# Two stacked products and a re-searched order in a one-core hybrid attention layer

## The chip, the cores and the metric

The kernel runs on one core of a Trainium2 chip. The metric is the time of one execution in microseconds (us), measured on the device; before the change the median of three runs is 308.2 us (308.15 to 308.23). Engines are named as the profile names them: PE is TensorE's matmul, PEld its loading of the stationary operand, DVE VectorE, ACT ScalarE, POOL GpSimd, SP SyncE, whose queue issues all the transfers here.

## The reference

One layer over x of 512 positions by 1024. After an RMS norm, one projection (1024 by 3420 columns) feeds two groups of eight heads of width 64, and one output projection and the residual end the layer. All in float32.

```
h = rms_norm(x, norm_gain);  proj = h @ w_in
# group A, two key groups g of four heads: three attentions share the queries
o_cmp = attend(qn, kc_cmp, vc_cmp)      # 31 compressed keys (blocks of 32, stride 16, through an MLP)
o_sel = attend(qn, ks_r, vs)            # blocks of 64 selected; 16 of 8 wanted, so all causal keys
o_win = attend(qn, kw_r, vw)            # window 512, so all causal keys
o_nsa = (g0*o_cmp + g1*o_sel + g2*o_win) * silu(z_n)
# group B: an indexer scores all keys, each query attends its best 128 causal keys
score = sum_h relu(qi_h . ki) * wi_h;   idx = top_k(score, 128)
o_dsa = attend(qd, kd[idx], vd[idx]) * silu(z_d)
out = x + concat(o_nsa, o_dsa) @ w_out
```

## The kernel before, in words

Every float32 operand of a matmul is split into two float32r parts, hi (the rounded value) and lo (what the rounding left), and a product is made as hi*hi + hi*lo + lo*hi, or with one exact side as two matmuls. The splitting of the weights is a cast on ACT and a subtraction on POOL (line L358); that of activations is a cast on ACT and a subtraction on DVE.

The projection is made in chunks of columns (C, B, Q1, Q2, D, Z0 to Z3; matmuls at L391 and L401), the output projection at L1268 (`out`). Attention goes by units: a unit is one kind (`n` group A, `d` group B), one block i of 128 query positions, one key group g, and for `n` one of three branches (0 compressed, 1 selected, 2 window). `n300` is kind n, i = 3, g = 0, branch 0. Inside a unit the queries stand as four row blocks b of 32 positions by four heads, 128 rows each. So row block b of query block i has 128 i + 32 b + 32 causal keys at most.

A unit runs so: scores `s_...` on PE (L1033), masked minimum on DVE (L1003), exponential on ACT (L1010), scaling on POOL (L1023) into `P_...`; then by tiles of 128 keys `transposed` turns P on PE into a bank `T_...` (L1054, four transposes of 128x128), casts it to `pth` on ACT (L1056) and subtracts it into `ptl` on DVE (L1057); `times_values` multiplies each of the two with the values on PE (L1068) into `on...` or `od...`. The values tile holds hi and lo side by side as 128 stationary columns, and `combine` adds the two halves.

Two tiles of this are the subject. First, the compressed branch: its P is 128 rows by 4 blocks by 32 keys. One transpose (L1045) makes a 128x128 bank whose rows are (block, key); DVE multiplies it with a block-diagonal mask `diag` into 128x512 (L1047), ACT casts (L1049), POOL subtracts (L1050), and two matmuls of 512 columns follow; the compressed values are held four times, once for every block. Second, the tile of 128 keys on the diagonal of a `d` unit, which is treated as every other tile, though blocks 0 and 1 have at most 64 keys in it.

The order on each engine is not that of the code: `set_order` takes the whole program, costs each instruction (`cost`), and lets list scheduling run forward and backward over it `ROUNDS` times; the order with the earliest planned end is fixed with dependencies. Buffers come from pools with tags: two tiles of one tag share memory, and the later waits for the last reader of the earlier. `arena` is one tile from which constants are carved; `cst` is the array of constants in DRAM. `tables` multiplies the rotary tables with a gain on POOL (L525, L526, tile `tab`); `rope` uses them; `nz` and `ny` are inverse norms made by a chain of small POOL operations (L417 to L424), and `dr_q` takes `nz` through DRAM to the layout of the softmax. `hid` is the hidden layer of the compression MLP, `kc_ps` its compressed keys on the way to `kn`, the stack of group A's keys.

Of the kernel before, what the change touches and what calls it, by code (L numbers as in the profile page):

```python
# [109 lines left out]
def set_order(tc):  # L110
# [66 lines left out]
    for k, i in enumerate(insts):  # L177
        acc = []
        for w, ap in aps(i):
            t = ap.bass_ap.tensor  # L180
# [4 lines left out]
            off += sum((n - 1) * st for st, n in dims[1:] if st < 0)
            acc.append((t.name, "PSUM" in str(getattr(t, "space", "")), w, p0, p0 + dims[0][1], off * size, end * size))
            if getattr(t, "tag", None):
                u = used.setdefault(t.name, [])
# [4 lines left out]
        for name, bank, w, p0, p1, a, b in acc:
            for j, w2, q0, q1, c, d in seen.get(name, ()):
                if (a <= d and c <= b) if bank else (w or w2) and a < d and c < b and p0 < q1 and q0 < p1:
                    (before if w or w2 or eng[j] != eng[k] else behind)[k].add(j)
# [113 lines left out]
def tile_hybrid_layer(ctx, tc, xT, x, ng, win, gains, peT, w1, b1, w2, wout, cst, out):  # L310
# [125 lines left out]

    tri = carve([S], BF16)
    nc.vector.memset(tri, 0.0)  # L440
# [71 lines left out]
    nc.gpsimd.tensor_copy(trib[:, 32:64], cs[:, C_TRIB:C_TRIB + 32])  # L512
    nc.gpsimd.tensor_copy(trib[:, S + 32:S + 64], cs[:, C_TRIB:C_TRIB + 32])
    nc.gpsimd.memset(trib[:, S + 64:S + 96], -NEG)
    ccos = cs[:64, C_CCOS:C_CCOS + HD]
# [4 lines left out]

    def tables(j, name):
        gn = gns[:, j, None, :]
        tab = work.tile([128, 2, NT, HD], F32, tag=f"tab{j}", name=f"tab{j}", bufs=1)
# [1 line left out]
        nc.gpsimd.tensor_tensor(c, cosd, gn[:, :, :HD].to_broadcast([128, NT, HD]), op=ALU.mult)  # L525
        nc.gpsimd.tensor_tensor(s, sind, gn[:, :, HD:].to_broadcast([128, NT, HD]), op=ALU.mult)  # L526
# [207 lines left out]
    diag = carve([4, 128], BF16)  # L734
    nc.gpsimd.memset(diag, 0.0)
    for h in range(4):
        nc.gpsimd.memset(diag[32 * h:32 * h + 32, h], 1.0)
# [60 lines left out]
    def hidden1(kv):  # L798
# [12 lines left out]
    def hidden2(kv):  # L811
        hid, uT = FSs[kv]
        if kv:
            for g in range(2):
                for half in range(2):
                    nc.tensor.matmul(hid[:, 384 + 64 * g:448 + 64 * g], uT[:, half, g].rearrange("p r c -> p (r c)"),
                                     w2t[:, kv, half], start=(half == 0), stop=(half == 1))
# [220 lines left out]
    def transposed(u, item, parts):  # L1038

        p = ps("T", "T_" + u.name)  # L1040
        ph = work.tile([128, 512], F32R, tag="pth", name="pth", bufs=TBUFS)
        pl = work.tile([128, 512], F32R, tag="ptl", name="ptl", bufs=TBUFS)
        if u.b == 0 and u.kind == "n":
# [3 lines left out]
            nc.vector.tensor_tensor(pd, p[:, None, :128].to_broadcast([128, 4, 128]), diag, op=ALU.mult)  # L1047
            pd = pd.rearrange("p h q -> p (h q)")
            nc.scalar.copy(ph, pd)  # L1049
            nc.gpsimd.tensor_tensor(pl, pd, ph.bitcast(F32), op=ALU.subtract)  # L1050
        else:
            blocks = item[0]
            for b, c in blocks:
                nc.tensor.transpose(p[:, b * 128:(b + 1) * 128], u.P[:, b, c:c + 128], ident)  # L1054
            cols = slice(128 * blocks[0][0], 512)
            nc.scalar.copy(ph[:, cols], p[:, cols])  # L1056
            nc.vector.tensor_tensor(pl[:, cols], p[:, cols], ph[:, cols].bitcast(F32), op=ALU.subtract)  # L1057
        parts.append((u, item, ph, pl))

    def times_values(u, item, *parts):  # L1060
# [5 lines left out]
        for cols, v in item[1]:  # L1066
            for x, pp in enumerate(parts):
                nc.tensor.matmul(o[:, cols], v, pp[:, cols], start=(first and x == 0), stop=(end and x == 1))  # L1068
# [261 lines left out]
    weave(att, "n002", [  # L1330
        queries("Q2", "q", 0, [1], "D", {0: hidden3(), 1: hidden1(1), 3: hidden2(1)},
                (e_first, lambda p, t: e_evac(p[:, 256:], t), lambda: norm_scale([ST["kd_raw"]], ST["ss_kd"]))),
        queries("D", "d", 3, [0, 1], "Z0"),
        kd_stack(),
    ], RA, X1, LEAD)
# [112 lines left out]
```

## Time and profile before

| what | before |
|---|---|
| median of three runs | 308.2 us |
| profiled execution, span from its first to its last instruction | 306.4 us |
| median less span | 1.8 us |
| PE busy | 301.3 us (98%), 1669 matmuls |
| PEld busy | 256.4 us (84%) |
| DVE / ACT / POOL busy | 261.0 (85%) / 240.7 (79%) / 235.4 us (77%) |
| chain that ended last, by engine | PE 86%, DVE 4%, ACT 4%, POOL 3%, DMA 2%, issue 1% |
| moved by DMA | 32.42 MB, mean 106 GB/s |
| TensorE clock granted | 0.999 of full |

The profile is of one execution, for which it gives the span alone; the 1.8 us to the median lie around the span. In rows of groups the columns are line, engine, operation, tiles (out<-in), shapes and count, then busy us and mean ns of one, then the engine's idle time just before and who ended it. Rows of a timeline give start us, us, engine, line. A matmul's duration holds its passage through the array, which overlaps with the next; what a matmul costs PE is the distance from its start to the next start.

### The profile page before, as it was taken

What the parts mean: (1) busy time and instruction counts of PE and PEld (TensorE: products, weight loads), DVE (VectorE), ACT (ScalarE), POOL (GpSimd) and SP (SyncE); (2) the same over time, 40 slices, a digit from 0 to 9 for tenths busy, and PEclk for the clock granted to TensorE, in tenths of its full rate; (3) what the DMA queues carried; (4) which work ended last, traced back from release to release, by engine and by line L of the source; (5) the groups of instructions that cost most, each with busy time, mean ns of one, the idle gap of its engine ahead of it and who ended that gap; (6) DMA issues with size and microseconds to landing.
All of it is one profiled execution on the core that took longest, in us unless ns stands there. A gap on an engine that the chain in (4) does not pass through costs nothing.

```text
span 306.4 us, 5994 instructions
## 1 busy us (share of the span) xinstructions
PE 301.3 (98%) x1669; PEld 256.4 (84%) x1669; DVE 261.0 (85%) x797; ACT 240.7 (79%) x802; POOL 235.4 (77%) x418
## 2 busy tenths in 40 slices
PE   8999999999999999999999999999999999999995
PEld 5997788899878878888888888888888888888885
DVE  4999699999979998998999999999769989986502
ACT  6965776798969999999989999774379998996400
POOL 3099899997996599987989879985667997686410
PEclk9999999999999999999999999999999999999999
DMA  7995345375410034310121023450443343003011
GB/s 282 415 356 181 96 147 163 92 187 158 114 28 0 0 79 125 106 57 3 38 68 39 3 72 106 136 165 0 141 125 120 106 141 103 4 14 122 20 50 68
DMA packets 21249, 32.42 MB, mean 106 GB/s; under 512 B 5664, under 2 KB 8480, under 8 KB 21216
## 3 DMA queue, kind: packets, MB, share of 16 engines
q1 hardware_dynamic: 21216, 32.05, 34.2%
q8 instruction: 13, 0.21, 0.3%
q14 instruction: 20, 0.16, 0.2%
HBM read 29.04 MB, written 2.47 MB: 103 GB/s over the span
## 4 chain that ended last, share of the span: by engine, by line
PE 86%; DVE 4%; ACT 4%; POOL 3%; DMA 2%; issue 1%; DVEq 0%; POOLq 0%
PE out L1268 15%; PE z L401 14%; PE Q L391 8%; PE D L391 7%; PE B L391 7%; PE on L1068 7%; PE s_n L1033 6%; PE T_n L1054 5%; PE od L1068 3%; PE T_d L1054 3%; PE s_d L1033 3%; PE C L401 2%; PE hid L787 2%; ACT hThi L467 2%; POOL wlo_Q L358 2%; PE idx L699 1%
## 5 line engine op out<-in xcount | busy, mean ns | idle before, releaser
L1010 ACT ACTIVATE P_n<-P_n,arena 128x416 f32<-128x416 f32 (+15 forms) x64 | 33.7, 528 | 4.7 <-DVE arena L1003 4.1
L1003 DVE CUSTOM_DVE_ANT_0 P_n<-s_n,arena 128x416 f32<-128x416 f32 (+15 forms) x64 | 31.0, 499 | 1.0 <-PE s_n L1033 0.4
L1023 POOL TENSOR_SCALAR P_n<-P_n,arena 128x416 f32<-128x416 f32 (+15 forms) x64 | 30.8, 501 | 1.2
L1057 DVE TENSOR_TENSOR ptl<-T_n,pth 128x512 fp32r<-128x512 f32 (+1 forms) x40 | 25.0, 627 | 3.6 <-ACT pth L1056 2.9
L1033 PE MATMUL s_n<-kn,arena_r 128*128 128x512 f32 (+11 forms) x104 | 27.1, 342 | 0.0
L710 DVE MAX8 m<-scores 128x8 f32<-128x512 f32 (+2 forms) x48 | 26.5, 552 | 0.6
L401 PE MATMUL z<-hThi,whi_Z 128*128 128x512 f32 x64 | 26.1, 408 | 0.0
L711 DVE MATCH_REPLACE8 scores<-m,scores 128x512 f32<-128x512 f32 (+2 forms) x48 | 26.0, 542 | 0.1
L401 PE MATMUL z<-hTlo,whi_Z 128*128 128x512 f32 x64 | 25.3, 396 | 0.0
L401 PE MATMUL z<-hThi,wlo_Z 128*128 128x512 f32 x64 | 25.2, 397 | 0.0
L1054 PE MATMUL T_n<-arena,P_n 128*128 128x128 f32 x144 | 24.1, 273 | 0.0
L1268 PE MATMUL out<-whi_wo,mx 128*128 128x512 f32 (+1 forms) x72 | 23.8, 374 | 0.0
L1268 PE MATMUL out<-wohi,mx 128*128 128x512 f32 (+1 forms) x72 | 23.7, 377 | 0.0
L1056 ACT CAST pth<-T_n 128x512 fp32r<-128x512 f32 (+1 forms) x40 | 21.5, 540 | 2.7 <-PE od L1068 1.6
L391 PE MATMUL Q<-whi_Q,hThi 128*128 128x256 f32 (+1 forms) x64 | 22.2, 347 | 0.6 <-DVE kn L587 0.6
L391 PE MATMUL Q<-wlo_Q,hThi 128*128 128x256 f32 (+1 forms) x64 | 21.9, 343 | 0.0
L391 PE MATMUL Q<-whi_Q,hTlo 128*128 128x256 f32 (+1 forms) x64 | 21.9, 344 | 0.0
L1054 PEld LDWEIGHTS T_n<-arena,P_n 128*128 128x128 f32 x144 | 18.1, 140 | 4.0
L1033 PEld LDWEIGHTS s_n<-kn,arena_r 128*128 128x128 f32 x104 | 18.1, 189 | 3.3 <-issue 0.2
L358 POOL TENSOR_TENSOR wlo_Z<-raw_Z,whi_Z 128x512 fp32r<-128x512 f32 x16 | 20.4, 1291 | 0.5 <-ACT whi_Z L357 0.5
L358 POOL TENSOR_TENSOR w1l<-raw_w,w1h 128x512 fp32r<-128x512 f32 x16 | 20.4, 1292 | 0.0
L1068 PE MATMUL on<-pth,arena_r 128*128 128x512 f32 (+1 forms) x48 | 18.3, 382 | 0.0
(270 smaller groups left out, 1108.1 us busy)
## 6 DMA issues: line engine op xcount, KB each, us to landing
raw_w<-in_w_dram SPq DMA_DIRECT2D x16, 256.0 KB, 3.7
raw_Z<-in_win_dram SPq DMA_DIRECT2D x16, 256.0 KB, 2.8
wor<-in_wout_dram SPq DMA_DIRECT2D x16, 256.0 KB, 2.8
raw_Q<-in_win_dram SPq DMA_DIRECT2D x12, 256.0 KB, 3.0
raw_D<-in_win_dram SPq DMA_DIRECT2D x8, 256.0 KB, 2.9
xres<-in_x_dram SPq DMA_DIRECT2D x8, 256.0 KB, 3.0
out_dram<-xres SPq DMA_DIRECT2D x7, 256.0 KB, 2.0
xw<-in_xT_dram SPq DMA_DIRECT2D x2, 860.0 KB, 7.8
```

The lines of the kernel that those rows point to most:

```text
L358: engine.tensor_tensor(lo, raw, hi.bitcast(F32), op=ALU.subtract)
L391: nc.tensor.matmul(out_ps, a[:, k, tsl], b, start=(k == 0 and b is hi and a is hT["hi"]), stop=(k == KB - 1 and a is hT["lo"]))
L401: nc.tensor.matmul(out_ps, b[:, csl], a[:, k, :], start=(k == 0 and b is hi and a is hT["hi"]), stop=(k == KB - 1 and b is lo))
L710: nc.vector.max(m8, sc)
L711: nc.vector.match_replace(sc, m8, sc, -3e30)
L1003: nc.vector.tensor_tensor_reduce(P, src_, mask, u.r[:, b:b + 1], 3e38, op0=ALU.add, op1=ALU.min, accum_out=m[:, b:b + 1])
L1010: nc.scalar.activation(P, P, AF.Exp, bias=m[:, b:b + 1], scale=-1.0, accum_out=l[:, b:b + 1])
L1023: nc.gpsimd.tensor_scalar(Pb, Pb, l[:, bb:bb + 1], 1.0 if u.gate is not None else 0.5, op0=ALU.mult, op1=ALU.mult)
L1033: nc.tensor.matmul(p, q[0][:, b], k[:, x], start=(x == 0), stop=(x == 1))
L1054: nc.tensor.transpose(p[:, b * 128:(b + 1) * 128], u.P[:, b, c:c + 128], ident)
L1068: nc.tensor.matmul(o[:, cols], v, pp[:, cols], start=(first and x == 0), stop=(end and x == 1))
L1268: nc.tensor.matmul(p, a, b[:, csl], start=(k == 0 and b is hi and a is mx[0]), stop=(k == 7 and a is mx[1]))
```

## The change

1. Compressed branch: four transposes of 128x32 instead of one of 128x128; ACT writes hi to rows 0 to 31 of `pth`, DVE writes lo to rows 32 to 63 of the same tile, and one matmul over 64 rows takes both. The values are held twice instead of four times, so `hid` for the values has 64 stationary columns instead of 128. `diag`, its five memsets, the multiplication and the subtraction on POOL go.
2. Diagonal tile of the `d` units: blocks 2 and 3 as before; for blocks 0 and 1 transposes of 128x64, hi in rows 0 to 63 and lo in rows 64 to 127 of `pth`, and one matmul of 256 columns against `vdd`, a copy of the values' first 64 rows in both halves, which two new transfers make after chunk Q2.
3. The constants come in two transfers; tables 3 and 4 share memory with 2 and 1; `rope`'s ring is 6 deep instead of 8; the arena is smaller.
4. `set_order`: 20 rounds instead of 8, other costs for PE, and two accesses to one PSUM bank are ordered whenever one of them writes.

```diff
-RTN, RTX = 8, 1
+RTN, RTX = 6, 1
-ROUNDS = 8
+ROUNDS = 20
         if e == "PE":
-            wide = len(ins) > 1 and str(ins[0].dtype).endswith("float32") and not i.is_transpose
-            return max(108, slow * n * (4 if wide else 1) * 0.432 + 10), 0
+            load = 0.845 * free(ins[1])
+            if i.is_transpose:
+                return max(28, load), 0
+            if str(ins[0].dtype).endswith("float32"):
+                return 2 * max(4 + load, 0.864 * n + 10), 0
+            return max(load, slow * n * 0.432 + 10), 0
...
-                if (a <= d and c <= b) if bank else (w or w2) and a < d and c < b and p0 < q1 and q0 < p1:
+                if (w or w2 or a <= d and c <= b) if bank else (w or w2) and a < d and c < b and p0 < q1 and q0 < p1:
...
-    cs = carve([C_TOT], F32)
-    nc.sync.dma_start(cs, cst)
+    cs = carve([C_COS], F32)
+    nc.sync.dma_start(cs, cst[:, :C_COS])
+    early = b8.tile([128, C_TOT - C_COS], F32, tag="early", name="early")
+    nc.sync.dma_start(early, cst[:, C_COS:])
...
-        tab = work.tile([128, 2, NT, HD], F32, tag=f"tab{j}", name=f"tab{j}", bufs=1)
+        tab = work.tile([128, 2, NT, HD], F32, tag=f"tab{j if j < 3 else 5 - j}", name=f"tab{j}", bufs=1)
...
-        rep = 4 if kv else 1
+        rep = 2 if kv else 1
-                    nc.tensor.matmul(hid[:, 384 + 64 * g:448 + 64 * g], uT[:, half, g].rearrange("p r c -> p (r c)"),
+                    nc.tensor.matmul(hid[:64, 384 + 64 * g:448 + 64 * g], uT[:, half, g].rearrange("p r c -> p (r c)"),
...
+    def e_done():
+        norm_scale([ST["kd_raw"]], ST["ss_kd"])
+        for x in range(2):
+            nc.sync.dma_start(vdd[64 * x:64 * x + 64].bitcast(F32),
+                              vd[0:64].rearrange("p t g s d -> p t g (s d)").bitcast(F32))
...
         if u.b == 0 and u.kind == "n":
-            nc.tensor.transpose(p[:, :128], u.P.rearrange("p h c -> p (h c)"), ident)
-            pd = work.tile([128, 4, 128], F32, tag="t2k", name="pd", bufs=2)
-            nc.vector.tensor_tensor(pd, p[:, None, :128].to_broadcast([128, 4, 128]), diag, op=ALU.mult)
-            nc.scalar.copy(ph, pd)
-            nc.gpsimd.tensor_tensor(pl, pd, ph.bitcast(F32), op=ALU.subtract)
+            for b in range(4):
+                nc.tensor.transpose(p[:32, b * 128:(b + 1) * 128], u.P[:, b], ident)
+            nc.scalar.copy(ph[:32], p[:32])
+            nc.vector.tensor_tensor(ph[32:64], p[:32], ph[:32].bitcast(F32), op=ALU.subtract)
+            parts.append((u, item, [(cols, v[:64], [ph[:64, cols]]) for cols, v in item[1]]))
+            return
...
+        if item[2:]:
+            c, lo_, v = item[2]
+            for b in range(2):
+                nc.tensor.transpose(p[:64, b * 128:(b + 1) * 128], u.P[:, b, c:c + 64], ident)
+            nc.scalar.copy(ph[:64, lo_], p[:64, lo_])
+            nc.vector.tensor_tensor(ph[64:, lo_], p[:64, lo_], ph[:64, lo_].bitcast(F32), op=ALU.subtract)
+            products.insert(0, (lo_, v, [ph[:, lo_]]))
...
         if kind == "d":
-            u.items = [tile_of(u, 128 * j, pair(vd[:, j, g])) for j in range(i + 1)]
+            u.items = [tile_of(u, 128 * j, pair(vd[:, j, g])) for j in range(i)]
+            u.items.append(([(b, 128 * i) for b in (2, 3)], [(slice(256, 512), pair(vd[:, i, g]))],
+                            (128 * i, slice(0, 256), vdd[:, i, g])))
```

How the order moves, at three places. A row is line, operation, tiles with their numbers, shape.

PE where the compressed unit n300 is transposed (`T_n300`) and the values' `hid` is made, among chunk Q2's matmuls; before:

```order
L1033 MATMUL s_n202_1872<-kn0_399,arena_r_73 128x320 x2
L391 MATMUL Q2_3_1771<-wlo_Q23_1131,hThi_74 128x512
L391 MATMUL Q2_3_1771<-whi_Q23_1130,hTlo_75 128x512
L391 MATMUL Q2_3_1771<-whi_Q23_1130,hThi_74 128x512
L1033 MATMUL s_n202_1998<-kn0_399,arena_r_73 128x384 x2
L391 MATMUL Q2_3_1771<-wlo_Q23_1131,hThi_74 128x512
L1045 MATMUL T_n300_1856<-arena_72 128x128
L1033 MATMUL s_n202_2003<-kn0_399,arena_r_73 128x384 x2
L391 MATMUL Q2_3_1771<-whi_Q23_1130,hTlo_75 128x512
L816 MATMUL hid1_1361<-arena_72,uT_1627 128x64 x4
```

The same place in the changed kernel:

```order
L1042 MATMUL s_n202_1872<-kn0_403,arena_r_73 128x320 x2
L1054 MATMUL T_n300_1856<-arena_72 32x128 x3
L394 MATMUL Q2_3_1771<-whi_Q23_1130,hThi_74 128x512
L1054 MATMUL T_n300_1856<-arena_72 32x128
L394 MATMUL Q2_3_1771<-wlo_Q23_1131,hThi_74 128x512
L1042 MATMUL s_n202_2000<-kn0_403,arena_r_73 128x384 x2
L394 MATMUL Q2_3_1771<-whi_Q23_1130,hTlo_75 128x512
L1042 MATMUL s_n202_2005<-kn0_403,arena_r_73 128x384 x2
L817 MATMUL hid1_1361<-w2t_401,uT_1627 64x64 x4
```

One wide transpose has become four narrow ones, three together and one behind a Q2 matmul; `hid` has half the rows.

PE where the products of the last two `d` units stand (od000 and od010), between matmuls of the output projection; before:

```order
L1268 MATMUL out11_4143<-whi_wo3_3340,mx_3979 128x512
L1068 MATMUL od000_4218<-pth_4168,arena_r_73 128x512
L1068 MATMUL od000_4218<-ptl_4169,arena_r_73 128x512
L1268 MATMUL out10_4142<-wohi_3350,mx_4017 128x512
L1268 MATMUL out10_4142<-wolo_3351,mx_4017 128x512
L1268 MATMUL out10_4142<-wohi_3350,mx_4017 128x512
L1068 MATMUL od010_4233<-pth_4187,arena_r_73 128x512
L1068 MATMUL od010_4233<-ptl_4188,arena_r_73 128x512
```

In the changed kernel:

```order
L1288 MATMUL out11_4156<-whi_wo3_3344,mx_3988 128x512
L1086 MATMUL od000_4234<-pth_4180,vdd_405 128x256
L1086 MATMUL od000_4234<-pth_4180,arena_r_73 128x256
L1086 MATMUL od000_4234<-ptl_4181,arena_r_73 128x256
L1288 MATMUL out10_4155<-wohi_3353,mx_4029 128x512
L1288 MATMUL out10_4155<-wolo_3354,mx_4029 128x512
L1288 MATMUL out10_4155<-wohi_3353,mx_4029 128x512
L1086 MATMUL od010_4250<-pth_4201,vdd_405 128x256
L1086 MATMUL od010_4250<-pth_4201,arena_r_73 128x256
L1086 MATMUL od010_4250<-ptl_4202,arena_r_73 128x256
```

Two matmuls of 512 columns have become three of 256, and nothing else moved here.

POOL ahead of the first attention unit, where the inverse norms `nz` of the first queries and the compressed keys `kscr` are made; before:

```order
L424 TENSOR_TENSOR nz_1335<-nwt_1338,nz_1335 128x16
L424 TENSOR_TENSOR ky_1230<-nkt_1234,ky_1230 64x1
L421 TENSOR_TENSOR nwt_1338<-nz_1335 128x16
L545 TENSOR_TENSOR kscr_1228<-rk12_1254,rk22_1252 64x64
L422 TENSOR_TENSOR nwt_1338<-nwt_1338,nwa_1339 128x16
L838 TENSOR_SCALAR kscr_1228<-kscr_1228,ky_1230 64x64
L423 TENSOR_SCALAR nwt_1338<-nwt_1338 128x16
L545 TENSOR_TENSOR R_q0_1143<-rt14_1331,rt24_1329 128x256
L424 TENSOR_TENSOR nz_1335<-nwt_1338,nz_1335 128x16
L358 TENSOR_TENSOR w1l14_1083<-raw_w114_1080,w1h14_1082 128x512
```

In the changed kernel:

```order
L361 TENSOR_TENSOR wlo_Q23_1131<-raw_Q27_1136,whi_Q23_1130 128x512
L427 TENSOR_TENSOR nz_1335<-nwt_1338,nwi_1337 128x16
L424 TENSOR_TENSOR nwt_1338<-nz_1335 128x16
L425 TENSOR_TENSOR nwt_1338<-nwt_1338,nwa_1339 128x16
L426 TENSOR_SCALAR nwt_1338<-nwt_1338 128x16
L427 TENSOR_TENSOR nz_1335<-nwt_1338,nz_1335 128x16
L424 TENSOR_TENSOR nwt_1338<-nz_1335 128x16
L425 TENSOR_TENSOR nwt_1338<-nwt_1338,nwa_1339 128x16
L530 TENSOR_TENSOR tab4_1458<-early_284,gns_291 128x256
L426 TENSOR_SCALAR nwt_1338<-nwt_1338 128x16
L427 TENSOR_TENSOR nz_1335<-nwt_1338,nz_1335 128x16
L531 TENSOR_TENSOR tab4_1458<-early_284,gns_291 128x256
```

The compressed keys have gone ahead of the last two splits of Q2, out of the chain of `nz`; the table `tab4`, which shares its memory with `tab1` now and stood 67 places earlier before, has come into it.

More of the change, by code (lines that the diff above doesn't have):

```diff
@@ L51 @@
 C_ID = 0
-C_COS = 128
+C_CMASK = C_ID + 128
+C_VALID = C_CMASK + 62
+C_COS = C_VALID + 4
 C_SIN = C_COS + NT * HD
 C_TRI = C_SIN + NT * HD
-C_CMASK = C_TRI + 128
-C_VALID = C_CMASK + 62
-C_TRIB = C_VALID + 4
+C_TRIB = C_TRI + 128
 C_CCOS = C_TRIB + 32
@@ L60 @@
 C_TOT = C_CSIN + HD
-ARENA = 3689 + 272 - 192
+ARENA = 3689 + 272 - 192 - 256 - 256 - 256 - (C_TOT - C_COS)
 ARENA_R = 5376 - 1024
 WARM = 10
-RTN, RTX = 8, 1
+RTN, RTX = 6, 1
 PD = 3
@@ L435, in rsqrt @@
             e.tensor_copy(y, cur)
-    tri = carve([S], BF16)
+    tri = b8.tile([128, S], BF16, tag="tri", name="tri")
     nc.vector.memset(tri, 0.0)
@@ L499, in tile_hybrid_layer @@
     x_stats()
-    cs = carve([C_TOT], F32)
-    nc.sync.dma_start(cs, cst)
+    cs = carve([C_COS], F32)
+    nc.sync.dma_start(cs, cst[:, :C_COS])
+    early = b8.tile([128, C_TOT - C_COS], F32, tag="early", name="early")
+    nc.sync.dma_start(early, cst[:, C_COS:])
     ident = cs[:, C_ID:C_ID + 128]
-    cosd = cs[:, C_COS:C_COS + NT * HD].rearrange("p (t d) -> p t d", t=NT)
-    sind = cs[:, C_SIN:C_SIN + NT * HD].rearrange("p (t d) -> p t d", t=NT)
-    nc.gpsimd.tensor_copy(tri[:, S - 128:S], cs[:, C_TRI:C_TRI + 128])
+    cosd = early[:, :NT * HD].rearrange("p (t d) -> p t d", t=NT)
+    sind = early[:, C_SIN - C_COS:C_TRI - C_COS].rearrange("p (t d) -> p t d", t=NT)
+    nc.gpsimd.tensor_copy(tri[:, S - 128:S], early[:, C_TRI - C_COS:C_TRIB - C_COS])
     cmask = cs[:, C_CMASK:C_CMASK + 62]
@@ L511, in tile_hybrid_layer @@
     nc.gpsimd.memset(trib, 0.0)
-    nc.gpsimd.tensor_copy(trib[:, 32:64], cs[:, C_TRIB:C_TRIB + 32])
-    nc.gpsimd.tensor_copy(trib[:, S + 32:S + 64], cs[:, C_TRIB:C_TRIB + 32])
+    nc.gpsimd.tensor_copy(trib[:, 32:64], early[:, C_TRIB - C_COS:C_CCOS - C_COS])
+    nc.gpsimd.tensor_copy(trib[:, S + 32:S + 64], early[:, C_TRIB - C_COS:C_CCOS - C_COS])
     nc.gpsimd.memset(trib[:, S + 64:S + 96], -NEG)
-    ccos = cs[:64, C_CCOS:C_CCOS + HD]
-    csin = cs[:64, C_CSIN:C_CSIN + HD]
+    ccos = early[:64, C_CCOS - C_COS:C_CSIN - C_COS]
+    csin = early[:64, C_CSIN - C_COS:]
     gns = b8.tile([128, 6, 2 * HD], F32, tag="gns", name="gns")
@@ L722, in tile_hybrid_layer @@
     nc.sync.dma_start(b1r, b1.rearrange("(o a) b -> o a b", o=1).partition_broadcast(64))
-    w2t = carve([2, 2, HD], F32)
+    w2t = b8.tile([128, 2, 2, HD], F32, tag="w2t", name="w2t")
     nc.sync.dma_start(w2t, w2)
@@ L733, in tile_hybrid_layer @@
     K_CMP, K_SEL = S, S + 32
[L734 to L737, printed above, removed]
     w1t = {}
@@ L802, in hidden1 @@
         src_ = hid[:, 256:384].rearrange("p (a g c) -> p a g c", a=2, g=2)
-        rep = 4 if kv else 1
-        uT = work.tile([128, 512], F32, tag="uT", name="uT", bufs=1)[:, :128 * rep]
+        rep = 2 if kv else 1
+        uT = work.tile([128, 256], F32, tag="uT", name="uT", bufs=1)[:, :128 * rep]
         uT = uT.rearrange("p (a g r c) -> p a g r c", a=2, g=2, r=rep)
@@ L841, in hidden2 @@
             for g in range(2):
-                c2 = hid[:, 384 + 64 * g:448 + 64 * g]
-                nc.scalar.activation(vcs[:, g, 0], c2, AF.Copy, scale=0.5)
-                nc.vector.scalar_tensor_tensor(vcs[:, g, 1], c2, 0.5, vcs[:, g, 0].bitcast(F32),
+                c2 = hid[:64, 384 + 64 * g:448 + 64 * g]
+                nc.scalar.activation(vcs[:64, g, 0], c2, AF.Copy, scale=0.5)
+                nc.vector.scalar_tensor_tensor(vcs[:64, g, 1], c2, 0.5, vcs[:64, g, 0].bitcast(F32),
                                                op0=ALU.mult, op1=ALU.subtract)
@@ L914, in tile_hybrid_layer @@
     vd = carve([NT, 2, 2, HD], F32R)
+    vdd = b8.tile([128, NT, 2, 2 * HD], F32R, tag="vdd", name="vdd")
     def e_first():
@@ L1041, in transposed @@
         ph = work.tile([128, 512], F32R, tag="pth", name="pth", bufs=TBUFS)
-        pl = work.tile([128, 512], F32R, tag="ptl", name="ptl", bufs=TBUFS)
-        if u.b == 0 and u.kind == "n":
-            nc.tensor.transpose(p[:, :128], u.P.rearrange("p h c -> p (h c)"), ident)
-            pd = work.tile([128, 4, 128], F32, tag="t2k", name="pd", bufs=2)
[L1047 to L1057, printed above, removed]
@@ L1058, in transposed @@
-        parts.append((u, item, ph, pl))
-    def times_values(u, item, *parts):
+        if u.b == 0 and u.kind == "n":
+            for b in range(4):
[4 more added lines that the diff above has]
+            return
+        pl = work.tile([128, 512], F32R, tag="ptl", name="ptl", bufs=TBUFS)
@@ new lines, in transposed @@
+        blocks = item[0]
+        for b, c in blocks:
+            nc.tensor.transpose(p[:, b * 128:(b + 1) * 128], u.P[:, b, c:c + 128], ident)
+        cols = slice(128 * blocks[0][0], 512)
+        products = [(cols, v, [ph[:, cols], pl[:, cols]]) for cols, v in item[1]]
+        if item[2:]:
[5 more added lines that the diff above has]
+            products.insert(0, (lo_, v, [ph[:, lo_]]))
@@ L1061, in times_values @@
+        nc.scalar.copy(ph[:, cols], p[:, cols])
+        nc.vector.tensor_tensor(pl[:, cols], p[:, cols], ph[:, cols].bitcast(F32), op=ALU.subtract)
+        parts.append((u, item, products))
+    def times_values(u, item, products):
         first = u.o[0] is None
@@ L1065, in times_values @@
         end = u.last and item is u.items[-1]
-        for cols, v in item[1]:
-            for x, pp in enumerate(parts):
-                nc.tensor.matmul(o[:, cols], v, pp[:, cols], start=(first and x == 0), stop=(end and x == 1))
+        for cols, v, moving in products:
+            done = end and (first or v is products[-1][1])
+            for x, pp in enumerate(moving):
+                nc.tensor.matmul(o[:, cols], v, pp, start=(first and x == 0), stop=(done and x == len(moving) - 1))
         if end:
@@ L1331, in tile_hybrid_layer @@
         queries("Q2", "q", 0, [1], "D", {0: hidden3(), 1: hidden1(1), 3: hidden2(1)},
[L1332 removed]
+                (e_first, lambda p, t: e_evac(p[:, 256:], t), e_done)),
         queries("D", "d", 3, [0, 1], "Z0"),
```

## The prediction

> **What bounds the kernel now.** I read the page first, then busy time by stretch, then the timeline of TensorE, then the groups by shape, the waits and the chain.
>
> ```profile
> span 306.4 us, 5994 instructions
> PE 301.3 (98%) x1669; PEld 256.4 (84%) x1669; DVE 261.0 (85%) x797; ACT 240.7 (79%) x802; POOL 235.4 (77%) x418
> ```
>
> ```profile
> core 0: us, PE busy (x) PEld busy (x) DVE busy (x) ACT busy (x) POOL busy (x), PEclk, DMA share, GB/s
> 60.00:92.00 32.00, 31.38 (x214) 28.34 (x213) 28.87 (x74) 27.44 (x111) 28.93 (x69) 1.00 0.46 124
> 92.00:120.00 28.00, 28.00 (x156) 23.59 (x157) 26.69 (x95) 27.29 (x98) 21.30 (x32) 1.00 0.18 48
> 228.00:286.00 58.00, 58.00 (x341) 49.83 (x340) 50.08 (x176) 51.15 (x170) 45.16 (x79) 1.00 0.28 88
> 286.00:306.40 20.40, 17.14 (x98) 14.86 (x96) 4.63 (x9) 2.63 (x7) 4.27 (x6) 0.98 0.14 51
> ```
>
> TensorE has work all the time: of 306.4 us it is idle 5.1, namely 1.2 before its first matmul, 3.3 after its last, and 0.6 in the stretch 60 to 92. A busy PE could still be slow, so the next rows ask whether it waits inside.
>
> ```profile
> 195.84 0.60 PE L1054 MATMUL T_d<-arena,P_d 128*128 128x128 f32 x4
> 196.19 0.48 PE L401 MATMUL z<-hThi,whi_Z 128*128 128x512 f32 x1
> 196.51 0.39 PE L401 MATMUL z<-hTlo,whi_Z 128*128 128x512 f32 x1
> 196.74 0.39 PE L401 MATMUL z<-hThi,wlo_Z 128*128 128x512 f32 x1
> ```
>
> A matmul of 512 columns costs 0.23 us (196.51 to 196.74). Four transposes with the matmul behind them take 195.84 to 196.51, 0.67, so the transposes cost 0.44, or 0.11 each. These steps hold all along; what the change takes off PE's list comes off the time one for one, unless another engine becomes late.
>
> **The change, part by part.** First the prices that the matmuls need.
>
> ```profile
> 28.78 0.40 PE L391 MATMUL B<-whi_B,hThi 128*128 128x512 f32 x1
> 29.01 0.27 PE L621 MATMUL qT_ps<-arena,ridx 128*128 128x128 f32 x1
> 29.04 0.48 PE L401 MATMUL C<-hThi,whi_C 128*128 128x512 f32 x1
> 29.36 0.39 PE L401 MATMUL C<-hTlo,whi_C 128*128 128x512 f32 x1
> ```
>
> ```profile
> 195.84 0.35 PEld L1054 LDWEIGHTS T_d<-arena,P_d 128*128 128x128 f32 x3
> 71.13 0.31 PEld L821 LDWEIGHTS hid<-arena,uT 128*64 128x64 f32 x4
> ```
>
> ```profile
> 117.87 1.00 PE L816 MATMUL hid<-arena,uT 128*128 128x64 f32 x8
> 118.68 0.36 PE L1068 MATMUL on<-pth,vm 128*128 128x256 f32 x1
> 118.88 0.28 PE L1068 MATMUL on<-ptl,vm 128*128 128x256 f32 x1
> 119.00 0.28 PE L1068 MATMUL on<-pth,arena_r 128*128 128x256 f32 x1
> ```
>
> A lone transpose costs 0.35 - 0.23 = 0.12 (29.01 to 29.36), yet the next matmul is taken up 0.03 after it. So the transpose itself occupies PE for 0.03, and the rest is the next load of 128 columns, which has nothing to hide behind. Loads of 128 columns follow each other in about 0.105 ((0.35 - 0.14) / 2, a load itself lasting 0.14), of 64 columns in 0.057 ((0.31 - 0.14) / 3). For 32 columns there is no row. Bounds: 0.03, the floor between the starts at 29.01 and 29.04, where halving 0.057 ends too, and 0.11, if the 128 rows that stream through set the pace and not the columns loaded. I take 0.03: it is what the array needed at 29.01. A matmul of 256 columns costs 0.12 (118.88 to 119.00).
>
> The Trainium skill, "TensorE: Matmul & The Clock Gate", section "LDWEIGHTS (loading the stationary operand)", has the load go by columns alone, columns / 1.2 ns, so 27 ns for 32; as an estimate from that page the sum below stays where it is. The trace has 57 ns for 64 columns where the page gives 53.
>
> Compressed units, 8 of them: one matmul of 512 columns goes, 8 x -0.23 = -1.84. One wide transpose (0.12) becomes four narrow ones: three at 0.03 and a last with the next load bare, 0.12; 8 x +0.09 = +0.72. In three units (n300, n100, n210) the order splits the four, and a bare load comes a second time: 3 x +0.09 = +0.27.
>
> Diagonal tiles, 8: two of 512 columns (0.46) become three of 256 (0.36), 8 x -0.10 = -0.80. Two of four transposes load 64 columns: 8 x 2 x (0.057 - 0.11) = -0.85. Values' `hid`: eight passes from 117.87 to 118.68, 0.10 each, come to 0.057: -0.35.
>
> Sum on PE: -1.84 + 0.72 + 0.27 - 0.80 - 0.85 - 0.35 = -2.85. With 0.11 for every narrow transpose: 8 x (4 x 0.11 - 0.12 - 0.23) - 0.80 - 0.35 = -0.4; the two ends are -2.9 and -0.4.
>
> The other engines:
>
> ```profile
> L1057 DVE TENSOR_TENSOR ptl<-T_d,pth 128x512 fp32r<-128x512 f32 x20 | 13.7, 686 | 4.2 <-ACT pth L1056 4.0
> L1056 ACT CAST pth<-T_d 128x512 fp32r<-128x512 f32 x20 | 11.6, 579 | 1.9 <-PE od L1068 1.1 <-PE T_d L1054 0.7
> L1050 POOL TENSOR_TENSOR ptl<-pd,pth 128x512 fp32r<-128x512 f32 x8 | 10.3, 1292 | 0.0
> L1047 DVE TENSOR_TENSOR pd<-T_n,arena 128x512 f32<-128x512 f32 x8 | 5.4, 680 | 0.1
> L1049 ACT CAST pth<-pd 128x512 fp32r<-128x512 f32 x8 | 4.9, 618 | 0.3 <-DVE pd L1047 0.3
> L1057 DVE TENSOR_TENSOR ptl<-T_n,pth 128x256 fp32r<-128x256 f32 x8 | 3.3, 416 | 0.6 <-ACT pth L1056 0.4
> L1056 ACT CAST pth<-T_n 128x256 fp32r<-128x256 f32 x8 | 2.9, 365 | 0.3 <-PE T_n L1054 0.2
> ```
>
> POOL loses L1050, 10.3 us. DVE trades the masking (680) for a subtraction of as many columns, ACT a cast (618) for one (579). In a diagonal tile one operation of 512 becomes two of 256: DVE 2 x 416 - 686 = +0.15, ACT 2 x 365 - 579 = +0.15, so 8 x 0.15 = +1.2 us on each. I cost it at nothing, since PE stands full beside ACT at 27.29 of 28 (row 92 to 120); in 228 to 286 ACT will have 51.15 + 6 x 0.15 = 52.1 of some 56, 93%. That is the cover, and a rival below prices its loss.
>
> The two `vdd` copies, 256 KB each, go to SP's queue between the fourth transfer of Z0's weights and the second `dr_q`.
>
> ```profile
> 128.66 2.80 SPq L1139 DMA_DIRECT2D mm<-dr_mask x4
> 141.85 0.34 SPq L667 DMA_DIRECT2D dr_q<-nz x1
> vm<-arena_r SPq DMA_DIRECT2D x2, 256.0 KB, 3.7
> ```
>
> SP issues nothing between 131.5 and 141.9 there, and the like copies `vm` landed in 3.7; the first diagonal product is 50 us later. Nothing. The split load of the constants puts the identity one transfer later, behind half of B: `cst` landed 11 us after its issue, some 10 us before its first use. The shallower ring of `rope` has POOL at most six additions behind DVE: nothing.
>
> **The order.** PE's 0.6 us of idling is one place:
>
> ```profile
> 91.04 0.28 PE L787 MATMUL hid<-w1h,FS 128*128 128x256 f32 x1
> 91.95 0.47 PE L391 MATMUL Q<-whi_Q,hThi 128*128 128x512 f32 x1 [0.62 <-DVE kn L587]
> DVE rt L539 <- DMA dr_q<-nz: 0.7, 1, 0.7
> 89.67 0.29 DVE rt L539
> 91.45 0.35 DVE arena_r L868
> 87.90 0.22 POOL nz L424
> ```
>
> A Q2 matmul waits for the bank of the first Q2 tile, which DVE empties late (91.45), since its `rt` waited 0.7 until `dr_q` had landed. In the new order, in rows of PE at the prices above, this matmul comes 1.1 us of PE work later, and the compressed keys come off POOL before the last two splits. I expect the idling gone, -0.6; but the order is new everywhere, and at T_n311 the product now stands 1.0 us behind its transposes, where ACT's cast alone takes 0.58: +0.2. Together -0.4, and between -0.6 and +1.0.
>
> **The sum.** -2.85 - 0.4 = -3.25 against the span: 306.4 becomes 303.15; with the 1.8 us around the span, 304.9 against the median of 308.2.
>
> **The rivals.**
>
> A: the rows streamed, not the columns loaded, set a narrow transpose's pace. For it: no row has fewer than 64 columns. Against: 29.01 to 29.04. Then -0.4 - 0.4, 307.4. Chance 0.11.
>
> B: ACT and DVE become the bound from 228 on, where 2.2 us of the 2.85 are to be gained. For it: 52.1 of 56 on ACT with every tile handed on twice. Against: 97% beside a full PE from 92 to 120. The gain there goes, 307.1. Chance 0.08.
>
> C, slower: POOL's shared tables.
>
> ```profile
> L525 POOL TENSOR_TENSOR tab<-arena,gns 128x256 f32<-128x256 f32 x5 | 3.2, 634 | 0.0
> L526 POOL TENSOR_TENSOR tab<-arena,gns 128x256 f32<-128x256 f32 x5 | 3.2, 632 | 0.0
> ```
>
> `tab4`, 2 x 0.63, now stands in the chain of `nz`, and DVE's `rt` on the first Q2 tile needs it; behind `rt` wait the bank, and with it PE. From `rt` to PE's matmul it was 2.3 us (89.67 to 91.95). PE comes there at about 92.3 now, so `tab4` must be there by 90.0; each us later is one us. `nz` was done at 88.1; with nine small operations of 0.16 less and 1.3 more, `tab4` is done about 88. The kernel is slower than before from 94 on, say 96: 304.9 + 6 = 310.9. Against: six us more on POOL have no row. Chance 0.07.
>
> D: the same page, section "Part 4: PE-mode transpose", says that transposes don't keep the full clock, for they don't count as PE's activity; the change has 24 matmul instructions more, all transposes.
>
> ```profile
> 1.18 4.38 PE L444 MATMUL I<-arena 128*128 128x512 bf16 x10 [1.18 <-DVE arena L446]
> ```
>
> A window at the clock of the start, 0.43 for a matmul that later costs 0.23, would cost half of those 4.4 us, 2.2: 307.1. Against: the clock is 1.00 in every stretch above, transposes and all. Chance 0.01.
>
> **How the numbers follow.** The forecast's own case, 303.8 to 306.4, has 0.70; A 0.11, B 0.08, C 0.07, D 0.01; 0.03 for what I don't see. The likeliest gives 304.9. The range reaches up to A and B, 307.4, and down to where the idling and a little more vanish, 303.8. A difference under 0.2%, 0.6 us, can't be told from none. Faster: 0.70 + B + D + half of A = 0.84; same: the other half of A and a little, 0.08; slower: C and a little, 0.08.
>
> **What would show it.** Right: 1693 matmuls; in the narrow groups starts 0.03 apart, in the 64-column ones 0.06; `od` products 0.12 apart; PE busy near 298 with idling inside under 0.5; POOL near 224. Wrong: narrow starts 0.11 apart (A); PE idle after 228 with `pth` or `ptl` as releaser (B); a gap near 92 that ends on `tab` (C); PEclk under 1.00 (D).

## The result, and the profile after

The changed kernel takes 313.2 us in the median (311.6 to 313.4, 4 runs) against 308.2 before: a ratio of 1.0149, 95% interval 1.0125 to 1.0172. It is slower by 1.5%, where 304.9 was forecast. Its profiled execution has a span of 311.4 us, 5.0 more than before.

The page of the changed kernel, its span and its busy times, and then busy time by stretch as it was shown of before:

```profile
span 311.4 us, 6066 instructions
PE 305.6 (98%) x1693; PEld 256.0 (82%) x1693; DVE 264.7 (85%) x805; ACT 242.5 (78%) x810; POOL 225.4 (72%) x405
```

```profile
22.00:60.00 38.00, 37.40 (x182) 31.12 (x181) 33.73 (x96) 26.29 (x78) 34.02 (x38) 1.00 0.48 150
60.00:92.00 32.00, 32.00 (x211) 28.59 (x211) 29.89 (x76) 27.61 (x112) 29.20 (x70) 1.00 0.41 117
92.00:120.00 28.00, 27.82 (x160) 23.01 (x159) 25.99 (x93) 26.26 (x94) 22.48 (x34) 1.00 0.14 39
228.00:286.00 58.00, 58.00 (x348) 48.91 (x347) 52.54 (x185) 52.88 (x178) 40.99 (x75) 1.00 0.26 83
286.00:311.40 25.40, 21.96 (x127) 19.03 (x125) 7.17 (x15) 5.26 (x15) 6.41 (x9) 1.00 0.12 43
```

PE still has work nearly all the time, at a granted clock of 1.00. Its busy time has grown by 4.3 us, where 3 us less was forecast, and its idle time by 0.6. So the main question is not who made PE wait, but what its own instructions cost. The timeline of PE answers it: a group of four narrow transposes in the first two rows, a stacked compressed product in the next three.

```profile
136.21 0.60 PE L1054 MATMUL T_n<-arena 128*32 128x128 f32 x4
136.56 0.48 PE L394 MATMUL D<-whi_D,hThi 128*128 128x512 f32 x1
...
141.19 0.40 PE L394 MATMUL D<-whi_D,hTlo 128*128 128x512 f32 x1
141.52 0.49 PE L1086 MATMUL on<-pth,arena_r 64*128 64x512 f32 x1
141.94 0.50 PE L394 MATMUL D<-whi_D,hThi 128*128 128x512 f32 x1
142.28 0.39 PE L394 MATMUL D<-wlo_D,hThi 128*128 128x512 f32 x1
```

Four transposes of 32 columns occupy 136.21 to 136.56, and their last starts the usual 0.03 ahead of the next matmul, so the other three stand 0.11 apart: exactly what transposes of 128 columns did. The product over 64 rows is worse. A step of 512 columns is 0.23; here the one before it takes 0.33 (141.19 to 141.52), it takes 0.42, and the one behind it 0.34 (141.94 to 142.28). Together that is 0.39 more than three ordinary steps, so one stacked product costs 0.62, more than the two of 0.23 that the kernel before issued. Over all eight the mean is 0.61.

The loads of the stationary operand at the same place show what is missing:

```profile
140.97 0.19 PEld L394 LDWEIGHTS D<-whi_D,hTlo 128*128 128x128 f32 x1
141.52 0.18 PEld L1086 LDWEIGHTS on<-pth,arena_r 64*128 64x128 f32 x1 [0.36 <-issue]
141.94 0.19 PEld L394 LDWEIGHTS D<-whi_D,hThi 128*128 128x128 f32 x1 [0.24 <-issue]
142.05 0.19 PEld L394 LDWEIGHTS D<-wlo_D,hThi 128*128 128x128 f32 x1
```

An ordinary load starts a matmul ahead: that of `hTlo` at 140.97, for the matmul of 141.19. The load of the 64-row operand, and that of the 128-row operand behind it, start only when their own matmul does (141.52, 141.94). Nothing hides them.

### The profile page after: what moved, and what is told of

Read it like the earlier page. It is cut to its first block, busy times and chain, and to the rows that moved or that the text cites. A ratio compares the mean times of both kernels' runs of the same rounds, so it can differ in the third digit from the quotient of the medians.

```text
span 311.4 us, 6066 instructions
## 1 busy us (share of the span) xinstructions
PE 305.6 (98%) x1693; PEld 256.0 (82%) x1693; DVE 264.7 (85%) x805; ACT 242.5 (78%) x810; POOL 225.4 (72%) x405
## 3 DMA queue, kind: packets, MB, share of 16 engines
HBM read 29.04 MB, written 2.47 MB: 101 GB/s over the span
## 4 chain that ended last, share of the span: by engine, by line
PE 88%; DVE 6%; ACT 2%; issue 1%; DMA 1%; DVEq 0%
PE out L1288 15%; PE z L404 13%; PE Q L394 11%; PE D L394 7%; PE B L394 7%; PE on L1086 6%; PE s_n L1042 5%; PE T_n L1062 5%; PE s_d L1042 3%; PE od L1086 3%; PE hid L788 3%; PE T_d L1062 2%; PE C L404 2%; DVE xsq L475 1%; PE idx L704 1%
## 5 line engine op out<-in xcount | busy, mean ns | idle before, releaser
L1019 ACT ACTIVATE P_n<-P_n,arena 128x64 f32<-128x64 f32 (+15 forms) x64 | 33.7, 528 | 2.3 <-DVE arena L1012 1.2
L1086 PE MATMUL on<-pth,arena_r 128*128 128x512 f32 (+2 forms) x48 | 18.7, 391 | 0.0
```

The source lines that it names most:

```text
L1019: nc.scalar.activation(P, P, AF.Exp, bias=m[:, b:b + 1], scale=-1.0, accum_out=l[:, b:b + 1])
L1086: nc.tensor.matmul(o[:, cols], v, pp, start=(first and x == 0), stop=(done and x == len(moving) - 1))
```

## The experiments

The theory at first, called P: the new matmuls cost what the steps above show, wherever they stand. Its rival, O: the new order makes the loss, by waits. Four kernels took the change apart.

**e1_order**: both stackings taken back, the rest of the change kept.

```diff
-RTN, RTX = 6, 1
+RTN, RTX = 5, 1
-            u.items = [tile_of(u, 128 * j, pair(vd[:, j, g])) for j in range(i)]
-            u.items.append(...)
+            u.items = [tile_of(u, 128 * j, pair(vd[:, j, g])) for j in range(i + 1)]
...   # transposed, hidden2, diag: as before the change
```

> The changed kernel with both stackings taken back (the products are those of before), so that the new order search, the shared tables and the split constants stand alone; rope's ring is 5 deep instead of 6, or it does not fit. Theory P (prices: a narrow transpose costs 0.11 us, a 64-row product 0.62 with what it does to its neighbours): the stacking made +2.9 of the +5.0, so 313.2 - 2.9 = 310.3, and no less than 308. Theory O (order: the new search made the loss, by waits): 313 or more.

Measured: 309.4 us (308.8 to 310.3), ratio 1.0043 (1.0026 to 1.0059). So something besides the stackings costs 1.3 us, but far from all; theory P's 310.3 was 0.9 too high.

**e2_diag**: the diagonal stacking alone, with the new search.

```diff
-            for b in range(4):
-                nc.tensor.transpose(p[:32, ...], u.P[:, b], ident)
+            nc.tensor.transpose(p[:, :128], u.P.rearrange("p h c -> p (h c)"), ident)
...   # mask, cast, subtraction and two products as before
```

> The changed kernel with the compressed branch of before (one wide transpose, mask, two products of 512 columns), the diagonal stacking and the new search kept. Theory P: 8 x (0.44 + 0.62 - 0.12 - 0.46) = 3.9 less, hid +0.2: 309.5. Theory O: 313 as it was.

Measured: 307.8 us (307.3 to 308.2), ratio 0.9991 (0.9979 to 1.0003). The compressed stacking makes the whole loss and more. Theory P's 309.5 was a miss by 1.7 us: PE doesn't idle between its first and its last matmul in this kernel, where the changed kernel idles 1.2 us there, which would be most of it. Against e1_order the diagonal stacking gains 0.5%, 1.6 us. Half of that lies in the `od` products themselves, whose steps sum to 10.00 us in e1_order and to 9.17 here; the other half lies elsewhere in the two orders.

**e3_compressed**: the compressed stacking alone.

> The changed kernel with the diagonal tile of before, the compressed stacking kept (16 rounds of the search instead of 20, which do not fit). Theory P: the diagonal stacking gains only its 0.8 us of products (its transposes of 64 rows cost what those of 128 do), so 313.2 + 0.8 = 314.0. The prediction's prices: 8 x (0.10 + 0.106) = 1.65 lost, 314.9.

Measured: 315.5 us (315.1 to 315.8), ratio 1.0241 (1.0221 to 1.0262), 1.5 above theory P's 314.0 and 0.6 above the 314.9 of the prediction's prices, so this run alone doesn't speak for P. This kernel has a wait of its own, in PE's waits:

```profile
PE T_n L1058 <- POOL P_n L1028: 1.4, 2, 1.2
```

PE comes to transposes whose P POOL has not scaled yet. But the changed kernel has other waits in its place, and PE idles 6.0 us in all here against 5.8 there. So this wait explains little of the 1.5, and the rest was not followed up.

**e4_pad128**: the product over 128 rows, the upper 64 of them zeros.

```diff
+    nc.gpsimd.memset(vcs[64:128].bitcast(F32), 0.0)
...
+            nc.gpsimd.memset(ph[64:128].bitcast(F32), 0.0)
-            parts.append((u, item, [(cols, v[:64], [ph[:64, cols]]) for cols, v in item[1]]))
+            parts.append((u, item, [(cols, v, [ph[:, cols]]) for cols, v in item[1]]))
```

> The changed kernel, but the compressed product takes 128 rows: rows 64 to 127 of pth and of the values are zeros (a memset on POOL in each unit). Theory P: the product takes 0.23 with its load hidden instead of 0.62, 8 x -0.39 = -3.1: 310.1. Rival R (the 64 rows are not what makes it slow, but for example its operand written by two engines or its place in the order): 0.42 stays, 313.2.

Measured: 311.7 us (311.3 to 312.0), ratio 1.0115 (1.0097 to 1.0134): 1.5 us less than the changed kernel by the medians, 1.0 by the ratios, where 3.1 were expected. The product does what was said: three of the eight take 0.23 now, and the five that stand right behind transposes 0.31 to 0.32, like any matmul of 512 columns there (0.32 at 29.04 in the prediction's rows). But the order came out anew, and PE waits for POOL, which it did not in the changed kernel:

```profile
PE T_n L1064 <- POOL P_n L1033: 1.0, 3, 0.6
```

In all PE idles 6.3 us instead of 5.8. How the rest of the 3.1 was lost was not followed up. More work on zeros is cheaper than 64 rows, as far as it can be told from two intervals that just meet; yet 0.44 for the four transposes and 0.23 for one product still are 0.09 more than the 0.12 and 0.46 of before, so by these prices the stacked compressed branch can't win on PE in either form.

**m1_prices**: the disputed prices by themselves.

> No layer is computed: matmuls and transposes of one kind follow each other on PE, sixteen of each, and the output is what is left in the banks. Theory P: a product of 512 columns takes 0.23 us over 128 rows and 0.42 over 64 rows, also without any change of rows between them (half the rate); where both alternate, about 0.61 + 0.23 a pair. Transposes of 128, 64 and 32 columns take 0.11 each. Rival R: the 0.42 is the price of changing between 128 and 64 rows, and sixteen of 64 rows in a run take 0.23 each. The prediction's price: narrow transposes 0.03 to 0.06.

Its timeline of PE (L142 are 128 rows, L146 64 rows, L148 32 rows, L150 96 rows; L152 and L153 alternate; L155 and L156 alternate between the lower and the upper 64 rows; L167, L169, L171 are float32 transposes of 128, 64 and 32 columns, L173 transposes of 64 rows, L183 of 32 columns in float32r):

```profile
13.26 3.79 PE L142 MATMUL k<-v,w 128*128 128x512 f32 x16
...
20.66 3.14 PE L146 MATMUL k<-v,w 64*128 64x512 f32 x13
23.73 3.94 PE L148 MATMUL k<-v,w 32*128 32x512 f32 x16
27.59 5.53 PE L150 MATMUL k<-v,w 96*128 96x512 f32 x16
...
33.29 0.49 PE L153 MATMUL k<-v,w 64*128 64x512 f32 x1
33.72 0.50 PE L152 MATMUL k<-v,w 128*128 128x512 f32 x1
34.15 0.50 PE L153 MATMUL k<-v,w 64*128 64x512 f32 x1
...
39.63 0.39 PE L155 MATMUL k<-v,w 64*128 64x512 f32 x1
39.63 0.62 PE L156 MATMUL k<-v,w 64*128 64x512 f32 x2
39.86 0.62 PE L155 MATMUL k<-v,w 64*128 64x512 f32 x2
...
57.56 1.91 PE L167 MATMUL k<-ident,P 128*128 128x128 f32 x16
59.31 1.91 PE L169 MATMUL k<-ident,P 128*64 128x128 f32 x16
61.06 1.91 PE L171 MATMUL k<-ident,P 128*32 128x128 f32 x16
62.90 1.21 PE L173 MATMUL k<-ident,P 64*128 64x64 f32 x16
64.04 0.49 PE L175 MATMUL k<-v,w 128*128 128x512 f32 x1
...
69.42 1.20 PE L183 MATMUL k<-identr,Pr 128*32 128x128 f32 x16
70.45 3.90 PE L185 MATMUL k<-v,w 128*128 128x512 f32 x16
```

The narrow transposes are settled: sixteen take 1.75 us at 128 columns (57.56 to 59.31) and 1.75 at 64, 0.109 each, and those of 32 columns end at 62.90 after 1.84, of which 0.1 is the change of rows behind them. What sets their pace is the 128 columns that stream: with 64 of them (L173) it is (64.04 - 62.90) / 16 = 0.07, the change of rows behind them included. In float32r the stream is nearly twice as fast, (70.45 - 69.42) / 16 = 0.064.

The 64-row product is not what theory P took it for. Thirteen of them in a row take 20.66 to 23.73, 0.236 each, the change at the end included: the rate is the full one. Where 64 and 128 rows alternate, a pair takes 33.29 to 34.15, 0.86, where two ordinary steps are 0.46. Two changes cost 0.40, one 0.20. Rival R is right.

The rows of L150 seem to say that 96 rows are slower, 5.37 us for sixteen (27.59 to 32.96). They are not: for most of these rows the granted clock was 0.50.

```profile
core 0: us, PE busy (x) PEld busy (x) DVE busy (x) ACT busy (x) POOL busy (x), PEclk, DMA share, GB/s
28.19:31.61 3.42, 3.42 (x10) 2.64 (x9) 0.00 (x0) 0.00 (x0) 0.00 (x0) 0.50 0.00 0
```

Inside that stretch the steps are 0.43, behind it 0.22 to 0.24, which is the full rate again. Why the clock fell there, with PE busy all the time, the trace doesn't show. All other prices here are read where it was 1.00.

Nor do 64-row products in opposite halves pay for a change: L155 and L156 run side by side. One of each starts at 39.63 and the next of each at 39.86, so a pair takes 0.23, the time of one. That was not tried in the layer.

The Trainium skill, "TensorE: Matmul & The Clock Gate", section "Why this matters for your kernels", gives a single matmul of 32 rows the time of one of 128; the rows of L148 agree as long as the neighbours have as few rows. Its section "Part 3: Packing small matmuls" has an item that lets a load run beside a matmul only where the row groups differ, though another sentence there adds loads into a background weight buffer. The trace agrees for opposite halves, where a load starts at 39.40 for a matmul at 39.63; but a load also starts early between equal rows, and doesn't where 128 rows and 64 meet.

**e10_twice**: the same in the kernel. Every 64-row product twice.

```diff
-            parts.append((u, item, [(cols, v[:64], [ph[:64, cols]]) for cols, v in item[1]]))
+            parts.append((u, item, [(cols, v[:64], [ph[:64, cols], ph[:64, cols]]) for cols, v in item[1]]))
```

> The changed kernel, but every stacked compressed product of 64 rows is issued twice in a row, so the compressed branch counts double. Theory C (change): what costs is the change between 128 and 64 rows; the second product of a pair adds 0.23, the first shows a step of 0.23 and the second one of 0.42: 313.2 + 8 x 0.23 = 315.0. Theory H (half rate, theory P's first reading): both steps are 0.42: 313.2 + 3.4 = 316.6.

Measured: 316.4 us (316.1 to 316.6), ratio 1.0264 (1.0248 to 1.0280). By the time alone this is H's number, and it would mislead. The search separated three of the eight pairs, and the five that stayed together read so:

```profile
193.73 0.39 PE L404 MATMUL z<-hThi,wlo_Z 128*128 128x512 f32 x1
194.05 0.73 PE L1086 MATMUL on<-pth,arena_r 64*128 64x512 f32 x2
194.70 0.50 PE L404 MATMUL z<-hThi,whi_Z 128*128 128x512 f32 x1
195.04 0.39 PE L404 MATMUL z<-hTlo,whi_Z 128*128 128x512 f32 x1
```

Two products take 0.65 (194.05 to 194.70), not 0.84; with their neighbours' surplus of 0.09 and 0.11 that is 0.85 for a pair against 0.61 for one. So 5 x 0.24 + 3 x 0.61 = 3.0 us more are expected from changes alone, and 3.1 were measured by the medians, 3.5 by the ratios. Both lie near H's 3.4 too, so it is the rows and not the time that decide: theory C holds.

**before_again and the shifted kernels**: one thing was in no theory. In e1_order no product is new, and PE waits no more than before, yet it is 1.3 us slower. Its long runs of 512-column matmuls stood 0.232 apart, in the kernel before 0.227.

> The kernel before, unchanged. In its first profile half of the 512-column steps took 0.227 us, in all the later kernels four in five took 0.232, which is worth about 1.3 us. If that belongs to the kernel (its addresses or its order), a second profile shows 290 steps of 0.228 or less again and a span of 306.4; if it belongs to the execution or the chip, under 110 and about 307.5.

Measured: 308.4 us, span 306.6, and 307 steps of at most 0.228 against 293 in the first profile. The pace belongs to the kernel. In the built programs, `hT` lies at an odd multiple of 128 bytes in all of them (its hi part at byte 33920 of a partition, 265 x 128). The weights lie at odd ones in the kernel before (chunk B from byte 154496, 1207 x 128), and with few exceptions at even ones in the kernels with the smaller arena (148224, 1158 x 128). (In chunks C and Z `hT` streams and the weights are loaded, in chunks B, Q and D the other way round; both are slower.)

```diff
-ARENA = 3689 + 272 - 192 - 256 - 256 - 256 - (C_TOT - C_COS)
+ARENA = 3689 + 272 - 192 - 256 - 256 - 256 - (C_TOT - C_COS) + 32
```

**e7_after_shift**, the changed kernel with these 128 bytes:

> The changed kernel with 128 bytes more in the arena and nothing else: the order on PE is the same row for row, but every tile behind the arena, the weights among them, lies 128 bytes further. In the kernel before hT (moving) and the weights (stationary) both lie at an odd multiple of 128 bytes, in all the new kernels hT at an odd and the weights at an even one. Theory A (address): long runs of 512-column matmuls settle at 0.227 us again instead of 0.232, about 200 steps x 5 to 6 ns: 312.0 to 312.3. Rival: the 0.232 has another cause, 313.2.

**e8_before_shift**, the kernel before with 128 bytes more:

> The kernel before with 128 bytes more in the arena: the same order, the weights moved from an odd to an even multiple of 128 bytes. Theory A: 308.1 + 200 x 0.006 = 309.2. Rival: 308.1.

Measured: e7 311.2 us (310.6 to 312.6), ratio 1.0107 (1.0083 to 1.0131), 1.3 us less than the change by the ratios; e8 309.9 (309.0 to 310.2), ratio 1.0052 (1.0036 to 1.0067), 1.6 us more than before. Chunk B in a long run of PE, first the changed kernel, first and last of 25 rows, then e7_after_shift, first and last of 19:

```profile
50.75 0.40 PE L394 MATMUL B<-whi_B,hThi 128*128 128x512 f32 x1
...
56.36 0.39 PE L394 MATMUL B<-whi_B,hThi 128*128 128x512 f32 x1
```

```profile
53.82 0.39 PE L394 MATMUL B<-whi_B,hThi 128*128 128x512 f32 x1
...
57.90 0.39 PE L394 MATMUL B<-whi_B,hThi 128*128 128x512 f32 x1
```

5.61 / 24 = 0.234 against 4.08 / 18 = 0.227. Over the 550 steps between two 512-column matmuls that stay under 0.25 the mean falls from 0.2318 to 0.2295, 1.3 us. The intervals of e7 and of the change just meet; e8 lies clear of its kernel, and so does e9_diag_shift below. That the shift makes the pace is shown from both sides; why it does is not.

**e5_right_prices**: the order search of the changed kernel told the chip's prices.

```diff
             if i.is_transpose:
-                return max(28, load), 0
+                return 108, 0
...
+            if n == 512 and list(ins[0].ap)[0][1] == 64:
+                return 620, 0
```

> The changed kernel, with the order search told what the chip takes: 0.108 us for every transpose and 0.62 for the 64-row product. The products stay, so theory P keeps their 3.6 us. If the waits of the new order (1.3 us more than before) come from the wrong prices, they go: 312.0; if not, 313.2.

Measured: 312.4 us (312.0 to 312.8), ratio 1.0142 (1.0127 to 1.0157). PE waits for nothing any more after its first matmul, where the changed kernel had this and twice 0.2 (1.0 us in all, only 0.4 more than the 0.6 before, and not the 1.3 more of the expectation):

```profile
PE rrow_ps L560 <- DVE arena L438: 0.6, 1, 0.6
```

But the gain of 0.8 us against the change's median is not resolved, for the two intervals overlap.

**e6_diag_right_prices**, the diagonal stacking with those prices:

> The diagonal stacking alone (as e2_diag), the order search told 0.108 us for every transpose. Theory P: e2_diag has 1.4 us in waits, some of which go: 307.0 to 307.8. Theory O (any new order costs): 308 or more.

Measured: 308.4 us (307.8 to 308.9), ratio 1.0004 (0.9994 to 1.0014). A miss, and theory O's number: no faster than e2_diag. The expectation counted 1.4 us of waits in e2_diag, but its profile has one wait of PE alone, the 1.2 us ahead of the first matmul, which every version has. So there was nothing to gain. Its transposes stand in 106 groups instead of 95, and behind each group a load is bare.

**e9_diag_shift**: the diagonal stacking alone, at the better address.

> The diagonal stacking alone (as e2_diag) with 128 bytes more in the arena. Theory A: 307.8 - 1.2 = 306.6, faster than both. Rival: 307.8.

Measured: 306.4 us (305.9 to 306.7), ratio 0.9941 (0.9928 to 0.9953). It is the one version that is faster than both kernels. Its page:

```profile
span 304.7 us, 6028 instructions
PE 300.2 (98%) x1677; PEld 257.3 (84%) x1677; DVE 262.2 (86%) x805; ACT 242.6 (80%) x810; POOL 235.7 (77%) x418
```

## Why the prediction was wrong

The bound was right: PE's list is nearly all of the time, and what is taken from it or added counts one for one. Two prices, that of the 64-row product and that of a narrow transpose, failed, and the arena was left out of the sum.

| term of the sum | forecast, us | measured on PE, us |
|---|---|---|
| compressed products, 8 | -1.84 | 8 x 0.61 - 16 x 0.233 = +1.15 |
| compressed transposes, 32 narrow for 8 wide | +0.72 + 0.27 | 2.58 - 0.21 = +2.37 |
| diagonal products (24 of 256 columns for 16 of 512) | -0.80 | all `od` products with their bare loads, 9.94 to 9.44: -0.50 |
| diagonal transposes of 64 columns | -0.85 | 1.26 - 16 x 0.083 = -0.07 |
| values' `hid` | -0.35 | -0.20 |
| waits | -0.4 | PE's idling 5.15 to 5.78: +0.6 |
| pace of the long runs | none | 550 x (0.2318 - 0.2297) = +1.2 |
| not assigned (the bare loads behind split groups among it) | | +0.4 |
| sum | -3.25 | +5.0 |

**"8 x -0.23 = -1.84"** failed most, by 3.0 us. The step priced the remaining product like any of 512 columns and gave it no bounds, though it has 64 rows, which no 512-column row of the profile had. The rows to bound it stood in the profile of before, at the first of the three places where its matmuls change rows:

```profile
69.04 0.28 PE L391 MATMUL Q<-whi_Q,hTlo 128*128 128x256 f32 x1
69.25 0.33 PE L801 MATMUL hid<-arena,scr 64*128 64x64 f32 x2
69.51 0.38 PE L787 MATMUL hid<-w1h,FS 128*128 128x256 f32 x1
69.74 0.28 PE L787 MATMUL hid<-w1l,FS 128*128 128x256 f32 x1
```

A matmul of 256 columns costs 0.12, but 0.21 ahead of the two 64-row transposes and 0.23 behind them: 0.20 of surplus at their edges, 8 x 0.20 = 1.6 us.

**"I take 0.03"**: of the two bounds for a narrow transpose, 0.03 and 0.11, the upper one was true, as rival A said; A alone would have given 307.4. The start at 29.04, 0.03 behind a transpose, was misread. It is a matmul that starts while the transpose still streams, and pays in its own step (0.32). A step between two starts is a price only within a series of equals, and the series of transposes stood 0.11 apart in every row. The time of a load, which the prediction took for the pace, isn't the bound here. The Trainium skill, "TensorE: Matmul & The Clock Gate", section "LDWEIGHTS (loading the stationary operand)", tells of the load alone, and what was worked out from it was no price of a transpose.

**The waits**: the stall at 91.95 went, as forecast. The new order brought others, the largest 0.6 at `rrow_ps`, at 25 us, which no place of the prediction looked at. The range for it, -0.6 to +1.0, held.

**The arena**: its new size was listed and costed at nothing, without a cover named. It moved the weights by an odd multiple of 128 bytes (154496 - 148224 = 49 x 128).

Of the rivals: B did not come, for PE has no idle time from 228 to 286. C came out at the sign but not the mechanism: there is no gap near 92, and PE is full from 60 to 92. D did not come, with the clock at 1.00. The counts held: 1693 matmuls, POOL 225.4, `od` products 0.12 apart. PE busy did not: 305.6 instead of near 298, with 1.2 us of idling inside instead of under 0.5. The chance of 0.08 for slower was too low, since the costs without a row were given to the favourable end of a range and the one that mattered had no range.

## What to carry to other kernels

On a full PE, price a matmul in the company it will have: a lone product over 64 rows among 128-row ones cost 0.61 instead of 0.23, so pad it to 128 rows or put such products together (two in opposite halves took the time of one). A transpose costs the columns that stream through it, not the columns loaded, so cutting one wide into four narrow ones costs four. After any change of memory sizes, compare the pace of the longest run of equal matmuls with that of before, since a shift of 128 bytes was worth as much here as a part of the change.

## What the runs showed of the hardware that was not expected

- A change between stationary operands of 128 and 64 rows costs 0.20 us, for no load runs ahead over it (0.86 for an alternating pair of 512 columns, 0.46 for two equal ones). In a row, products over 64, 32 and 96 rows run at the full rate, 0.22 to 0.24 each at a clock of 1.00; pairs of 64-row products in opposite halves take 0.23 together.
- Float32 transposes stream at 0.109 us for 128 columns, whether they load 128, 64 or 32, those in float32r (32 loaded) at 0.064.
- Long runs of float32r matmuls of 512 columns settled at 0.227 in the kernels where both operands lie at odd multiples of 128 bytes, and stayed at 0.232 where one is odd and one even. No position but these was run, and the cause is open.
- The granted clock fell to 0.50 for 3.4 us (28.19 to 31.61 of m1_prices) while PE was busy without a break.
